# The split of a pair's fourth column sum, issued before or after the next coefficients' split

## The chip, the cores and the metric

The kernel runs on one core of one Trainium2 chip. The metric is the device time of one execution in microseconds, as the median of several runs. A core has five engines that each work through their own list of instructions in order and wait for one another through semaphores: TensorE (PE, with its weight loads shown as PEld), VectorE (DVE), ScalarE (ACT), GpSimd (POOL) and SyncE (SP, which here only issues DMAs).

## What is computed

The reference is a two-layer trunk. Each layer has a token mixer with cross-attention and a layer norm, and then PEER, a channel mixer over 128 x 128 = 16384 experts, with a second layer norm. The change touches only the last part of PEER, the sum over experts of coefficient times value row:

```python
def peer_ffn(x, w_q, subkeys, u_tab, v_tab):
    ...
        gw = jax.nn.softmax(fv, axis=-1)
        u = u_tab[eid]
        act = jax.nn.gelu(jnp.einsum('nhkd,nd->nhk', u, xb).astype(jnp.float32), approximate=False)
        coef = (gw * act).astype(x.dtype)
        return jnp.einsum('nhk,nhkd->nd', coef, v_tab[eid])
```

The kernel doesn't gather rows. It holds a dense coefficient for every expert and token (zero where a token did not pick the expert) and multiplies these coefficients with the whole table `v`, for 256 tokens and 1024 columns.

## The kernel before

**Precision.** A float32 product is made from three products in a shorter type. Each operand is split into a high part (a cast on ACT) and a low part (operand minus high part, a subtraction on DVE), and `mm3` (lines 182 to 186) issues high x high (L184), high x low (L185) and low x high (L186) into one PSUM bank. In the trace every product of the value pass has one of these three lines.

**The value pass** is the loop `for i in range(P)` at line 1276, run once in each of the two layers. Chunk `i` has 128 experts: their coefficients are a block of 128 x 256 (128 experts, 256 tokens), their value rows a block of 128 x 1024. What one turn of the loop issues, in the order in which it is written, is also the order on each engine, since the schedule is manual:

1. `self.next` (line 1279) pumps the split of the value rows two chunks ahead: the cast `wH` on ACT (L110) and the subtraction `wL` on DVE (L125). The pump also issues on SP the DMA that fills the next free raw buffer (L139).
2. `coef(i + 2)` (line 1295) splits the coefficients of the same chunk ahead: the cast `cH` on ACT (L246), the subtraction `cL` on DVE (L247).
3. `paired(i)` (line 1296) does what the pairs below need on ACT and DVE.
4. The products of chunk `i` on PE: for an ordinary chunk four outputs (two token halves by two column halves) of three 128x512 products each. Then come products owed by a pair.

`wH`, `wL`, `cH` and `cL` have three buffers each (`HL_BUFS`), so that the cast of chunk i + 2 into `wH` has to wait until PE is done with chunk i - 1.

**Pairs.** Every six chunks, two neighbouring chunks are multiplied as a 2 x 2 matrix product with seven multiplications instead of eight (the Strassen-Winograd form): `PAIRS` (line 39) lists the first chunk of each pair, 8, 14, ... 98 in layer 0 (16 pairs) and 8, 14, ... 104 in layer 1 (17 pairs). One of the seven products is made in the first chunk's own turn (`m1`, 3 matmuls), two in the second chunk's (6 matmuls). The other four need sums of coefficient blocks and sums of value blocks. `paired` forms these sums on DVE into places of coefficients that are used up, and in later turns splits them: the four coefficient sums into `sh` and `sl`, the four column sums into the tiles `th` and `tl`, which are the first six rows of `xHL`. There are three rows of `th` for four column sums, so the fourth (`t4`) goes into row 0 again once the product that read row 0 is made. The four owed products are three matmuls each and are placed by lines 1242 to 1246: where another pair follows at chunk n, product 0 comes at the end of turn n - 1, products 1 and 2 at the end of turn n, and product 3, the one that uses the fourth column sum, at the end of turn n + 1:

```python
                for m, at in enumerate((n - 1, n, n, n + 1) if n else (p + 4, p + 5, p + 5, p + 5)):
                    owed.setdefault(at, []).append((p, m))
                due[n or p + 5] = p
```

`due` says in which turn the fourth column sum is split: turn n, the first chunk of the next pair, and turn p + 5 behind the last pair of a layer. So it happens 16 times in layer 0 and 17 times in layer 1. In the trace this split is the ACT cast on L1194 and the DVE subtraction on L1195 (both 128x512, writing `xHL`), and product 3 is the group of three matmuls `bank<-xHL` whose second (L185) reads the low part that L1195 writes.

Other lines that the prediction names: L1212 and L1213 are the last two DVE sums of the next pair (in turn n - 1), L1184 a DVE split of a later turn.

Of the kernel before, what the change touches and what calls it, by code (L numbers as in the profile page):

```python
# [50 lines left out]
class Trunk:  # L51
# [986 lines left out]
    def peer_layer(self, layer):  # L1038
        nc, tc, A = self.nc, self.tc, self.A
        with ExitStack() as ctx:  # L1040
# [121 lines left out]
            th, tl = self.xHL[:, 0:3, :], self.xHL[:, 3:6, :]  # L1162
            sh, sl = self.xHL[:, 6, :], self.xHL[:, 7, :]
            plain = lambda a: a.bitcast(F32)
# [4 lines left out]
            def old(p, b, n):  # L1169
                t = lo if p + 6 < CLOSE - 2 else hi  # L1170
                return t[:, b:b + n, :].rearrange("p a b -> p (a b)")

            def sums_c(p):
                return old(p, 0, 2)

            def sums_r(p):
                return [old(p, 2, 4), old(p, 6, 2), old(p, 8 + 2 * (first[p] % 2), 2)]

            def paired(i):
                if i - 2 in first:  # L1180
                    c, (t13, _, _) = sums_c(i - 2), sums_r(i - 2)
                    nc.scalar.copy(sh, c)
                    nc.scalar.copy(th[:, 0:2], t13.rearrange("p (f a) -> p f a", f=2))
                    nc.vector.tensor_sub(sl, c, plain(sh))  # L1184
                if i - 3 in first:
                    t13, t2, _ = sums_r(i - 3)
                    nc.scalar.copy(th[:, 2], t2)
                    nc.vector.tensor_sub(tl[:, 0:2], t13.rearrange("p (f a) -> p f a", f=2), plain(th[:, 0:2]))
                if i - 4 in first:
                    _, t2, _ = sums_r(i - 4)  # L1190
                    nc.vector.tensor_sub(tl[:, 2], t2, plain(th[:, 2]))
                if i in due:
                    _, _, t4 = sums_r(due[i])
                    nc.scalar.copy(th[:, 0], t4)  # L1194
                    nc.vector.tensor_sub(tl[:, 0], t4, plain(th[:, 0]))  # L1195
                if i + 3 in first:
                    (ta, ua), (tb, ub) = part(i + 3), part(i + 4)
                    s = four(sums_c(i + 3))
                    nc.scalar.copy(s[:, 3], ub)
                    nc.vector.tensor_sub(s[:, 1], ta, ua)  # L1200
                    nc.vector.tensor_sub(s[:, 2], ub, s[:, 1])
                    nc.vector.tensor_add(s[:, 0], ua, ub)
                    nc.vector.tensor_sub(ub, tb, s[:, 2])
                if i + 2 in first or i + 1 in first:
                    t13, t2, t4 = sums_r(i + 2 if i + 2 in first else i + 1)
                    t1, t3 = t13[:, :512], t13[:, 512:]
                    (a0, a1), (b0, b1) = [[r[:, :512], r[:, 512:]] for r in self.pair]
                    if i + 2 in first:
                        nc.vector.tensor_sub(t1, a1, a0)
                        nc.vector.tensor_sub(t3, b1, a1)  # L1210
                    else:
                        nc.vector.tensor_add(t2, t3, a0)  # L1212
                        nc.vector.tensor_sub(t4, b0, t2)  # L1213
                        self.n_flight -= 2
                        self.load(len(self.items))
                q = hi[:, 0:2, :].rearrange("p a b -> p (a b)")

                def onto(t, h, src, scale=ALPHA):
                    xs = self.x[:, t, 512 * h:512 * h + 512]
                    nc.vector.scalar_tensor_tensor(xs, xs, scale, src, op0=ALU.mult, op1=ALU.add)  # L1220
                n = i - done
                if n == 1:
                    nc.scalar.copy(q, m1)
                    onto(0, 0, m1)
                elif n == 2:
                    nc.vector.tensor_add(q, q, m6)
                elif n == 3:
                    onto(0, 1, q)
                elif n == 4:
                    onto(0, 1, m5, 1.0)  # L1230
                elif n == 5:
                    nc.vector.tensor_add(q, q, m7)
                elif n == 6:
                    onto(1, 0, q)
                elif n == 7:
                    onto(1, 1, q)
                elif n == 8:
                    onto(1, 1, m5, 1.0)
# [3 lines left out]
            owed, due = {}, {}  # L1242
# [5 lines left out]
            def mixed(out, mh, ml, stat, k=None):  # L1248
                self.mm3(out, *stat, mh, ml, k == PAIRS[layer][0], k == PAIRS[layer][-1])

            def coef(i):
                src = block(i)
                if i in first:
                    cH, cL = cp.tile([P, T], F32R, name="cH"), cp.tile([P, T], F32R, name="cL")
                    self.split_to(cH[:, :P], cL[:, :P], src[:, :P])
                    return cH, cL
                pool, z = (ends, i - P + kept) if layer and i >= P - kept else (cp, "")
                cH = pool.tile([P, T], F32R, name=f"cH{z}")
                cL = pool.tile([P, T], F32R, name=f"cL{z}")
                self.split_to(cH, cL, src)  # L1260
                return cH, cL
# [8 lines left out]
            def products(tt, c0, n, part):  # L1270
                t = slice(tt * P, (tt + 1) * P)
                k, o = divmod(c0, 512)
                for i_, (h, l), (cH, cL) in part:
                    self.mm3(y[tt][k][:, o:o + n], cH[:, t], cL[:, t], h[:, c0:c0 + n], l[:, c0:c0 + n],
                             i_ == 0, i_ == P - 1)
            for i in range(P):
                if i + 2 > P - 1:
                    self.pool_cols = 512
                late.append((i, self.next(min(HL_BUFS, P - i)), cs.pop(0)))
                if i + 2 == CLOSE:  # L1280
                    right.close()
                    if layer == 0:
                        kv = self.later.enter_context(tc.tile_pool(name="kv1", bufs=1, side="right"))
                        self.memctx = self.later.enter_context(ExitStack())
                        m = self.memctx.enter_context(tc.tile_pool(name="mem1", bufs=1, side="right"))
                        self.mem_dest(kv, m)
                        m.tile([P, 80], F32, name="gap")
                        self.kvw = [(m.tile([P, D], F32R, name=f"kH{c}"), m.tile([P, D], F32R, name=f"kL{c}"))
                                    for c in range(4)]
                    else:  # L1290
                        ends = right.enter_context(tc.tile_pool(name="ends", bufs=1, side="right"))
                        self.extra = [(ends.tile([P, D], F32R, name=f"eH{e}"), ends.tile([P, D], F32R, name=f"eL{e}"))
                                      for e in range(EXTRA)]
                if i + 2 < P:
                    cs.append(coef(i + 2))
                paired(i)
                if i + 1 > P - kept:
                    continue
                if i in first or i - 1 in first:
                    (_, (h, l), (cH, cL)), = late  # L1300
                    if i in first:
                        mixed(m1, h[:, :512], l[:, :512], (cH[:, :P], cL[:, :P]), i)
                    else:
                        mixed(y[0][0], h[:, :512], l[:, :512], (cH[:, :P], cL[:, :P]))
                        mixed(y[0][1], h[:, 512:], l[:, 512:], (cH[:, P:], cL[:, P:]))
                else:
                    for tt in range(2):
                        for k in range(2):
                            products(tt, 512 * k, 512, late)
                for p, m in owed.get(i, ()):  # L1310
                    stat = four(sh)[:, m], four(sl)[:, m]
                    if m == 3:
                        mixed(y[1][0], th[:, 0], tl[:, 0], stat)
                    else:
                        mixed((m5, m7, m6)[m], th[:, m], tl[:, m], stat, p)
                late = []
# [175 lines left out]
```

## Time and profile before

| | |
|---|---|
| time, median of 3 runs | 1816.91 us (1815.43 to 1816.98) |
| profiled execution | 1813.94 us, of which the span from first to last instruction is 1812.2 us |
| mean granted TensorE clock | 0.999 |
| bytes moved | 334.24 MB, 184 GB/s over the span |

The value pass is the stretch from about 575 to 850 us (layer 0) and from about 1460 us to the end (layer 1). In a timeline, each row gives the start, the duration, the engine, the line, the operation with what it writes and reads, and in brackets the idle time of the engine ahead of it with what ended that idle time. A view of waits gives who waited for whom, with the total, the number of times and the longest one. The ends of matmuls are modelled, so that their durations overlap; their starts are what shows the rate.

### The profile page before, as it was taken

To read this page: it belongs to the slowest core of one execution; us is meant where nothing else is said; L and a number is where in the kernel's file an instruction comes from. 1 tells how busy PE (TensorE), PEld (TensorE's weight loads), DVE (VectorE), ACT (ScalarE), POOL (GpSimd) and SP (SyncE) were. 2 spreads that over 40 slices of the span, in tenths; PEclk is the share of its full clock that TensorE was granted. 3 is DMA by queue.
4 is the path that set the end of the run, shared out by engine and by line. 5 is a ranking of instruction groups with operands and counts; after the bars stand their busy time and mean duration, and the time that the engine had idled before them with its cause. 6 is when DMAs were issued, how large, how long until landed. Compare 5 with 4: busy or idle time off the path is not lost.

```text
span 1812.2 us, 33806 instructions
## 1 busy us (share of the span) xinstructions
PE 1792.1 (99%) x12711; PEld 1644.4 (91%) x12711; DVE 1489.2 (82%) x3081; ACT 1010.0 (56%) x1781; POOL 430.1 (24%) x324
## 2 busy tenths in 40 slices
PE   8999999999999999999999999999999999999998
PEld 8999999999999788888898899999999988888886
DVE  6684779599998999998868748685999989999977
ACT  6554555455544666666657355555554456666653
POOL 2015762333332000000101368325333300000000
PEclk9999999999999999999999999999999999999999
DMA  7556565655555555665756355665555555555564
GB/s 248 201 160 201 165 199 189 194 174 161 159 162 164 195 193 203 209 202 179 261 178 187 113 177 179 198 191 185 163 162 163 163 186 200 197 192 189 198 200 137
DMA packets 95557, 334.24 MB, mean 184 GB/s; under 512 B 10652, under 2 KB 13728, under 8 KB 95136
## 3 DMA queue, kind: packets, MB, share of 16 engines
q1 hardware_dynamic: 93752, 328.93, 56.6%
q10 hardware_dynamic: 1640, 3.15, 0.5%
q8 instruction: 99, 1.62, 0.4%
q14 instruction: 66, 0.54, 0.1%
HBM read 330.98 MB, written 1.05 MB: 183 GB/s over the span
## 4 chain that ended last, share of the span: by engine, by line
PE 72%; issue 17%; POOL 7%; DVE 2%; ACT 1%; DMA 0%; POOLq 0%; SPq 0%; DVEq 0%; ACTq 0%
PE bank L185 23%; PE bank L186 23%; PE bank L184 23%; POOL wL L120 7%; PE bank L250 2%; ACT wH L110 0%; DVE eL L125 0%; DVE wL L125 0%; PE bank L344 0%; DVE eH L110 0%; POOL wL L123 0%; PE bank L243 0%; DMA cp<-in_rg_par_dram 0%; DMA raw<-in_w0kg_dram 0%; DVE x L297 0%
## 5 line engine op out<-in xcount | busy, mean ns | idle before, releaser
L110 ACT CAST wH<-raw 128x1024 fp32r<-128x1024 f32 (+3 forms) x605 | 612.1, 1013 | 674.8 <-PE bank L186 191.8
L184 PE MATMUL bank<-xHL,wH 128*128 128x256 f32 x2536 | 715.0, 282 | 4.8 <-ACT wH L110 4.8
L186 PE MATMUL bank<-xHL,wL 128*128 128x256 f32 x2536 | 702.2, 277 | 0.5 <-DVE wL L125 0.5
L185 PE MATMUL bank<-xHL,wH 128*128 128x256 f32 x2536 | 702.0, 277 | 0.0
L125 DVE TENSOR_TENSOR wL<-raw,wH 128x1024 fp32r<-128x1024 f32 (+3 forms) x413 | 447.9, 1087 | 236.9 <-ACT wH L110 235.9
L184 PEld LDWEIGHTS bank<-xHL,wH 128*128 128x128 f32 x2536 | 476.9, 188 | 4.8 <-ACT wH L110 4.8
L186 PEld LDWEIGHTS bank<-xHL,wL 128*128 128x128 f32 x2536 | 476.7, 188 | 1.3 <-DVE wL L125 0.7
L185 PEld LDWEIGHTS bank<-xHL,wH 128*128 128x128 f32 x2536 | 477.5, 188 | 0.0
L185 PE MATMUL bank<-wL,cH 128*128 128x512 f32 x850 | 331.1, 390 | 0.4 <-DVE wL L125 0.4
L186 PE MATMUL bank<-wH,cL 128*128 128x512 f32 x850 | 330.5, 389 | 0.0
L184 PE MATMUL bank<-wH,cH 128*128 128x512 f32 x850 | 330.5, 389 | 0.0
L123 POOL TENSOR_TENSOR wL<-raw,wH 128x1024 fp32r<-128x1024 f32 (+1 forms) x121 | 255.6, 2115 | 209.8 <-ACT wH L110 209.1
L120 POOL TENSOR_TENSOR wL<-raw,wH 128x386 fp32r<-128x386 f32 x126 | 129.5, 1028 | 280.1 <-DVE wL L118 280.1
L185 PEld LDWEIGHTS bank<-wL,cH 128*128 128x128 f32 x850 | 159.5, 188 | 34.9 <-DVE wL L125 1.3
L186 PEld LDWEIGHTS bank<-wH,cL 128*128 128x128 f32 x850 | 159.6, 188 | 33.7
L184 PEld LDWEIGHTS bank<-wH,cH 128*128 128x128 f32 x850 | 159.6, 188 | 33.6
L1000 DVE TENSOR_TENSOR oh<-iota,i12T 128x1024 f16<-128x1024 f16 x128 | 130.4, 1019 | 0.0
L333 POOL TENSOR_TENSOR x<-x,raw 128x256 f32<-128x256 f32 x6 | 4.9, 823 | 467.2 <-ACT x L330 467.2
L118 DVE TENSOR_TENSOR wL<-raw,wH 128x640 fp32r<-128x640 f32 x126 | 104.0, 825 | 7.7 <-ACT wH L110 0.3
L1003 DVE TENSOR_TENSOR oh<-oh,gT 128x1024 f16<-128x1024 f16 x128 | 90.0, 703 | 4.4
L1133 PE MATMUL bank<-oh 128*128 128x128 f16 x1024 | 80.9, 220 | 1.1 <-DVE oh L1003 1.1
L1133 PEld LDWEIGHTS <-oh 128*128 128x128 f16 x1024 | 58.8, 97 | 6.0 <-DVE oh L1003 1.5
(339 smaller groups left out, 2122.5 us busy)
## 6 DMA issues: line engine op xcount, KB each, us to landing
raw<-in_u_dram SPq DMA_DIRECT2D x256, 512.0 KB, 3.6
raw<-in_v_dram SPq DMA_DIRECT2D x256, 512.0 KB, 4.5
raw<-in_w_q_dram SPq DMA_DIRECT2D x32, 512.0 KB, 4.2
raw<-in_w_out_dram SPq DMA_DIRECT2D x16, 512.0 KB, 4.0
raw<-in_w0qx_dram SPq DMA_DIRECT2D x8, 512.0 KB, 5.1
raw<-in_wkv_dram SPq DMA_DIRECT2D x8, 512.0 KB, 5.5
raw<-in_w0v_dram SPq DMA_DIRECT2D x8, 384.0 KB, 5.1
raw<-in_w0o_dram SPq DMA_DIRECT2D x8, 384.0 KB, 3.0
```

The lines of the kernel that those rows point to most:

```text
L110: (nc.vector.tensor_copy if self.cast_dve else nc.scalar.copy)(h[:, c], r[:, c])
L118: nc.vector.tensor_sub(l[:, k:], r[:, k:], h[:, k:].bitcast(F32))
L120: nc.gpsimd.tensor_sub(l[:, :k], r[:, :k], h[:, :k].bitcast(F32))
L123: nc.gpsimd.tensor_sub(l[:, :k], r[:, :k], h[:, :k].bitcast(F32))
L125: rest = lambda l=l, r=r, h=h, c=slice(k, n): nc.vector.tensor_sub(l[:, c], r[:, c], h[:, c].bitcast(F32))
L184: mm(out, sH, mH, start=start, stop=False, skip_group_check=True)
L185: mm(out, sH, mL, start=False, stop=False, skip_group_check=True)
L186: mm(out, sL, mH, start=False, stop=stop, skip_group_check=True)
L250: self.nc.tensor.matmul(out, lhsT, rhs, start=start, stop=stop, skip_group_check=True)
L1000: nc.vector.tensor_tensor(flat(oh[:, 1:3]), self.iota2.unsqueeze(1).to_broadcast([P, 4, P, 2]), pairs(self.i12T[:, j]), op=ALU.is_equal)
L1003: nc.vector.tensor_tensor(flat(oh[:, 0:2]), two.rearrange("p z (q e t) -> p z q e t", q=2, t=2), pairs(self.gT[:, j]), op=ALU.mult)
L1133: nc.tensor.matmul(wp[:, qs], oh[:, 2, q // 2, :, q % 2], oh[:, z, q // 2, :, q % 2], start=z == 0, stop=z == 1, skip_group_check=True)
```

## The change

The three statements that split the fourth column sum leave `paired` and go into the loop itself, ahead of `coef(i + 2)`. Nothing else changes: the same instructions with the same operands, in another order.

```diff
@@ in paired(i)
                 if i - 4 in first:
                     _, t2, _ = sums_r(i - 4)
                     nc.vector.tensor_sub(tl[:, 2], t2, plain(th[:, 2]))
-                if i in due:
-                    _, _, t4 = sums_r(due[i])
-                    nc.scalar.copy(th[:, 0], t4)
-                    nc.vector.tensor_sub(tl[:, 0], t4, plain(th[:, 0]))
@@ in the loop over chunks
+                if i in due:
+                    _, _, t4 = sums_r(due[i])
+                    nc.scalar.copy(th[:, 0], t4)
+                    nc.vector.tensor_sub(tl[:, 0], t4, plain(th[:, 0]))
                 if i + 2 < P:
                     cs.append(coef(i + 2))
                 paired(i)
```

The order of each engine's instructions after the change: on ACT, in the 33 turns concerned, `wH`, fourth sum's cast, `cH` instead of `wH`, `cH`, fourth sum's cast; on DVE `wL`, fourth sum's subtraction, `cL` instead of `wL`, `cL`, fourth sum's subtraction. The orders of PE, POOL and SP are the same. Among the waits, the first and third matmul of chunk n + 2 (L184 and L186) now carry waits of their own for `cH` and `cL`; before, the wait of product 3 on the later L1195 had covered them. The subtraction of the fourth sum waits for ACT alone, as before, and its cast waits for PE, as before.

## The prediction

> **What bounds the kernel now.** I read the busy times first, then the waits of PE's weight loads, then the timelines of PE, DVE and ACT around one pair.
>
> ```profile
> span 1812.2 us, 33806 instructions
> PE 1792.1 (99%) x12711; PEld 1644.4 (91%) x12711; DVE 1489.2 (82%) x3081; ACT 1010.0 (56%) x1781; POOL 430.1 (24%) x324
> ```
>
> PE is the bound, so this change can only pay where PE's stream has holes. A modelled matmul end can cover a short hole, so "99%" doesn't say that there are none. The weight loads (PEld) show them better. In their view of waits the longest total is this row:
>
> ```profile
> PEld bank L185 <- DVE xHL L1195: 11.6, 31, 0.4
> ```
>
> L1195 is the moved subtraction. In 31 places PE's second matmul of product 3 waits for it, 0.37 us each (11.6 / 31). There are 33 fourth sums; the two that don't appear are the last of each layer. Now PE's matmuls and weight loads at the first of the 31, and the matmuls at the last:
>
> ```profile
> 615.05 0.40 PE L184 MATMUL bank<-wH,cH 128*128 128x512 f32 x1
> 615.28 0.39 PE L185 MATMUL bank<-wL,cH 128*128 128x512 f32 x1
> 615.51 0.39 PE L186 MATMUL bank<-wH,cL 128*128 128x512 f32 x1
> 615.74 0.40 PE L184 MATMUL bank<-xHL 128*128 128x512 f32 x1
> 616.08 0.50 PE L185 MATMUL bank<-xHL 128*128 128x512 f32 x1
> 616.42 0.40 PE L186 MATMUL bank<-xHL 128*128 128x512 f32 x1
> 616.65 0.40 PE L184 MATMUL bank<-wH,cH 128*128 128x512 f32 x1
> ```
>
> ```profile
> 615.28 0.19 PEld L186 LDWEIGHTS bank<-wH,cL 128*128 128x128 f32 x1
> 615.52 0.19 PEld L184 LDWEIGHTS bank<-xHL 128*128 128x128 f32 x1
> 616.08 0.19 PEld L185 LDWEIGHTS bank<-xHL 128*128 128x128 f32 x1 [0.38 <-DVE xHL L1195]
> 616.19 0.19 PEld L186 LDWEIGHTS bank<-xHL 128*128 128x128 f32 x1
> 616.89 0.19 PEld L186 LDWEIGHTS bank<-wH,cL 128*128 128x128 f32 x1
> ```
>
> ```profile
> 1739.80 0.40 PE L184 MATMUL bank<-xHL 128*128 128x512 f32 x1
> ...
> 1740.72 0.39 PE L184 MATMUL bank<-wH,cH 128*128 128x512 f32 x1
> ```
>
> A group of three without a stall takes 615.74 - 615.05 = 0.69 us, 0.23 each. Product 3 takes 616.65 - 615.74 = 0.91 us at the first place and 1740.72 - 1739.80 = 0.92 at the last. So a stall costs PE **0.22 us**, not the 0.37 of the wait row: the load that waited would have started at about 615.52 + 0.23 = 615.75 and started at 616.08, 0.33 late, but the next load follows after only 0.11 (616.19), so that 0.11 of the delay is made up. All 31 together cost 31 x 0.22 = 6.8 us. Why the subtraction is late, on DVE:
>
> ```profile
> 613.26 0.69 DVE L1213 TENSOR_TENSOR wglo<-raw,wglo 128x512 f32<-128x512 f32 x1
> 613.87 1.22 DVE L125 TENSOR_TENSOR wL<-raw,wH 128x1024 fp32r<-128x1024 f32 x1
> 615.01 0.42 DVE L247 TENSOR_TENSOR cL<-wglo,cH 128x256 fp32r<-128x256 f32 x1
> 615.34 0.69 DVE L1195 TENSOR_TENSOR xHL<-wglo,xHL 128x512 fp32r<-128x512 f32 x1
> 615.94 1.22 DVE L125 TENSOR_TENSOR wL<-raw,wH 128x1024 fp32r<-128x1024 f32 x1
> ...
> 620.68 1.23 DVE L125 TENSOR_TENSOR wL<-raw,wH 128x1024 fp32r<-128x1024 f32 x1 [1.11 <-ACT wH L110]
> ```
>
> DVE works here without a gap. It is behind because the next pair's sums have just been made, and L1195 stands in its queue behind `cL`, which PE needs only later. L1195 ends at 615.34 + 0.69 = 616.03 and PE's load starts 0.05 later.
>
> **The change part by part.**
>
> *DVE.* L1195 goes ahead of `cL`. It can start where `cL` starts now, 615.01, if its input is there, and ends at 615.01 + 0.69 = 615.70, that is 0.33 earlier. With the same 0.05 to PE, the load may start at 615.75, just where it would come without any stall. Even a load at 615.75 + 0.11 = 615.86 would lose nothing, so there is 0.11 us of reserve. The order of two neighbours doesn't change DVE's total: `wL` of the next chunk still starts at 615.94.
>
> *Its input.* The cast on ACT moves ahead of `cH`:
>
> ```profile
> 612.79 0.41 ACT L246 CAST cH<-wglo 128x256 fp32r<-128x256 f32 x1
> 613.10 0.62 ACT L1194 CAST xHL<-wglo 128x512 fp32r<-128x512 f32 x1
> 613.62 1.04 ACT L110 CAST wH<-raw 128x1024 fp32r<-128x1024 f32 x1
> ...
> 619.59 1.05 ACT L110 CAST wH<-raw 128x1024 fp32r<-128x1024 f32 x1 [0.82 <-PE bank L186]
> ```
>
> ```profile
> 612.05 0.39 PE L186 MATMUL bank<-xHL 128*128 128x512 f32 x1
> ```
>
> It would start at 612.79 and end at 613.41, 1.60 us before DVE gets to it. It overwrites row 0 of `th`, which product 0 reads until 612.05 + 0.39 = 612.44; that is 0.35 before 612.79, so its wait for PE still costs ACT nothing. If it did cost something, `cH` and the next `wH` cast would queue behind it, and DVE's `cL` and `wL` behind those. The cast that follows at 613.62 keeps its time.
>
> *What is later.* `cH` starts 0.52 later (613.62 - 613.10), at 613.31, and ends at 613.72, long before DVE's `cL`. `cL` starts 0.60 later (615.94 - 615.34), at 615.61, and ends at 616.03. PE needs it for the load of the third matmul of chunk n + 2, now at 616.89, and 0.22 earlier, at 616.67, once the stall is gone: 0.59 us to spare. That margin is what hides the move; without it PE would stall there. The two new waits on PE for `cH` and `cL` are therefore met when PE comes to them, and I price them at nothing. The nearest row is a load that waited, which started 0.05 after its release; an already met wait has no such delay, and the opposite end, 0.05 at both matmuls of all 33 turns, would be 3.3 us. I take zero, because 0.05 is the price of an operand that comes late, and both operands are there over half a microsecond early.
>
> *Queues.* SP's next DMA goes out when `wL` is done:
>
> ```profile
> 615.12 0.33 SPq L139 DMA_DIRECT2D raw<-in_v_dram  x1
> ```
>
> `wL` ends at 615.09 and comes first in both orders, so no transfer moves. POOL has nothing here, and DVE's 1.11 us of idle at 620.68, ended by ACT and that by PE, shows that the engines start again from PE after each pair: a PE that is 0.22 earlier takes them along and only shortens that idle time.
>
> *The two last fourth sums* (turn p + 5) have no stall to lose; the first of them, and the matmul that reads it:
>
> ```profile
> 851.05 0.68 DVE L1195 TENSOR_TENSOR xHL<-wghi,xHL 128x512 fp32r<-128x512 f32 x1
> ```
>
> ```profile
> 853.32 0.39 PE L185 MATMUL bank<-xHL 128*128 128x512 f32 x1
> ```
>
> It ends at 851.73, 1.59 us early, so being earlier gains nothing.
>
> *Bounds.* The trace doesn't show the subtraction in its new place. At the late end it starts where it does now, 615.34, and the gain is zero. At the early end it starts at 615.01 and the whole stall goes; more than 0.22 per place can't be had from it. I take the early end: in this stretch each DVE instruction starts when its predecessor's row is about to end (615.01 against 613.87 + 1.22 = 615.09), whichever it is, and the input is 1.60 us early. Halfway, at 615.17, the load would come at 615.91, only 0.05 past the reserve. The bounds of the sum are 0 and 31 x 0.22 = 6.8 us.
>
> *A rule that speaks against it.* The Trainium skill, "TensorE: Matmul & The Clock Gate", section "Step-by-step: what each phase is for", says that PE can pull a weight load ahead of matmuls in flight. By that, only the matmul would have waited here, whose turn was 615.97: 0.11 late at 616.08, so the stalls would be worth 31 x 0.11 = 3.4 us in place of 6.8. The trace disagrees: the load of the waiting matmul itself starts at 616.08, and the starts behind it lose 0.22.
>
> **The sum.** 31 x 0.22 = 6.8 us less than the profiled execution's 1813.94 is 1807.1. The median of the runs shown, 1816.91, lies 3.0 above that execution; the change doesn't touch what differs between them, so I forecast 1816.91 - 6.8 = **1810.1 us**.
>
> **Rivals.**
>
> *Half of it.* PE's wait goes only in part: the subtraction reaches PE 0.22 later than worked out (0.33 gained less 0.22 leaves 0.11, and with it half of the stall), or a new wait at chunk n + 2 gives back half. 31 x 0.11 = 3.4, that is 1813.5. For it: PE has two waits that it did not have. Against: reserves of 0.11 and 0.59 us, and the 31 places are alike to a few hundredths in the rows above.
>
> *No change.* The stall only moves: PE comes 0.22 earlier and waits as long for `cL`. For it: `cL` becomes 0.60 later on an engine without a gap. Against: the 0.59 that remain. Or the stall isn't bound to the order: DVE could be held at L1195 by something that the view puts down to nothing. 1816.9.
>
> *Slower.* The cast carries a wait for PE and ACT works in order. If in its new place it were released not by product 0 (612.44) but only after all products of turn n + 1 up to 615.51 + 0.39 = 615.90, it would end at about 616.6, the subtraction at 617.3 and PE's load would start at 617.4 in place of 615.75, 1.65 late, 1.54 after the 0.11: a loss of 1.54 - 0.22 = 1.32 more than now, 31 x 1.32 = 41 us, 1858. It decides from the point at which the cast ends after 615.34 (the old start of the subtraction). Against: now it runs at 613.10, before turn n's products are done, so its wait is for product 0 alone, and PE's order is unchanged.
>
> **How the numbers follow.** Forecast 0.80, half 0.09, no change 0.07, slower 0.04. About 0.2% (3.6 us, a bound at 1813.3) is what a measurement of this kernel can tell from no change. The half lies on that bound and is split evenly: faster 0.80 + 0.04 = 0.84, same 0.05 + 0.07 = 0.12, slower 0.04. The range goes from the profiled execution's 1807.1, a little rounded down for spread, to the half's 1813.5: 1806.8 to 1813.6. It leaves out no change and slower, and the spread of the runs (1.5 us) fits in it.
>
> **What would show it right or wrong.** Right: the view of waits has no row of PEld L185 on the moved subtraction, or one of a few tenths in all; product 3's three starts are 0.23 apart; the subtraction starts right behind `wL` and `cL` 0.60 behind it; DVE's idle time before the L125 after a pair falls from 1.11 to about 0.9; the span is 6 to 7 us shorter. Wrong: PEld waits of similar total on L247 at chunk n + 2 (no change), an ACT row with idle time ahead of the moved cast (slower), or a wait of 0.1 to 0.2 us at the old place (half). A granted clock under the present one would make the prediction wrong for another reason:
>
> ```profile
> 616.00:632.00 16.00, 16.00 (x70) 12.87 (x69) 14.71 (x26) 10.27 (x18) 0.00 (x0) 1.00 0.61 195
> ```

## The result, and the profile after

The changed kernel takes 1809.11 us (median of 7 runs, 1808.74 to 1810.27), the kernel before 1815.43 us (median of 7 runs, 1814.63 to 1816.98). The ratio is 0.9965, with a 95% interval of 0.9954 to 0.9977: 6.3 us less, against the 6.8 forecast (1810.1 us).

First the view of waits of PE's weight loads in the changed kernel, the three rows that name the moved subtraction or what was put behind it:

```profile
PEld bank L184 <- ACT cH L246: 0.8, 1, 0.8
PEld bank L185 <- DVE xHL L1293: 0.3, 1, 0.3
PEld bank L186 <- DVE cL L247: 0.2, 1, 0.2
```

L1293 is the moved subtraction (L1195 before). One wait of 0.3 us is left of 31 that took 11.6 us. The single waits for `cH` and `cL` lie at 1785.92 and 1787.21 us, in a stall near the end that is far from the 33 turns concerned; in those turns no load waits for either. DVE at the first pair:

```profile
615.07 1.22 DVE L125 TENSOR_TENSOR wL<-raw,wH 128x1024 fp32r<-128x1024 f32 x1
616.20 0.69 DVE L1293 TENSOR_TENSOR xHL<-wglo,xHL 128x512 fp32r<-128x512 f32 x1
616.80 0.42 DVE L247 TENSOR_TENSOR cL<-wglo,cH 128x256 fp32r<-128x256 f32 x1
617.14 1.22 DVE L125 TENSOR_TENSOR wL<-raw,wH 128x1024 fp32r<-128x1024 f32 x1
...
621.67 1.23 DVE L125 TENSOR_TENSOR wL<-raw,wH 128x1024 fp32r<-128x1024 f32 x1 [0.90 <-ACT wH L110]
```

The subtraction starts 1.13 us behind the start of `wL`, in the place that `cL` had, and ends at 616.89. The next `wL` starts 2.07 us after the previous one (617.14 - 615.07), as before (615.94 - 613.87), so that the swap costs DVE nothing. The idle time at the end of the burst is 0.90 in place of 1.11. Now PE's weight loads and matmuls at product 3:

```profile
616.72 0.19 PEld L184 LDWEIGHTS bank<-xHL 128*128 128x128 f32 x1
616.94 0.19 PEld L185 LDWEIGHTS bank<-xHL 128*128 128x128 f32 x1
617.18 0.19 PEld L186 LDWEIGHTS bank<-xHL 128*128 128x128 f32 x1
```

```profile
616.94 0.40 PE L184 MATMUL bank<-xHL 128*128 128x512 f32 x1
617.17 0.39 PE L185 MATMUL bank<-xHL 128*128 128x512 f32 x1
617.40 0.40 PE L186 MATMUL bank<-xHL 128*128 128x512 f32 x1
617.64 0.40 PE L184 MATMUL bank<-wH,cH 128*128 128x512 f32 x1
```

The group takes 617.64 - 616.94 = 0.70 us instead of 0.91. It is the same in the other places: over the 31, the group takes 0.90 to 0.92 us in the trace before, and 0.69 or 0.70 in the changed one, but for two of 0.73 and 0.83. The load for L185 at the first place comes 0.22 behind the one ahead of it, at the very moment (616.94) that the subtraction's result can reach PE (616.89 + 0.05).

The mean granted clock is 0.999 in both profiles. The two profiled spans are only 3.7 us apart:

```profile
span 1808.5 us, 33773 instructions
```

The same matmul near the start of the value pass shows where the rest is. It stands twice in each trace, once per layer; first the kernel before, then the changed one:

```profile
600.69 0.50 PE L185 MATMUL bank<-wL,cH 128*128 128x512 f32 x1 [0.22 <-DVE wL L125]
```

```profile
1485.36 0.50 PE L185 MATMUL bank<-wL,cH 128*128 128x512 f32 x1 [0.22 <-DVE wL L125]
```

```profile
601.90 0.50 PE L185 MATMUL bank<-wL,cH 128*128 128x512 f32 x1 [0.22 <-DVE wL L125]
```

```profile
1483.53 0.50 PE L185 MATMUL bank<-wL,cH 128*128 128x512 f32 x1 [0.22 <-DVE wL L125]
```

Up to the first mark, ahead of any changed instruction, the profiled execution of the changed kernel was 1.2 us slower (601.90 - 600.69). From mark to mark it is 884.67 - 881.63 = 3.0 us faster (15 stalls of 0.22 would be 3.3), and from the second mark to the end 326.84 - 324.97 = 1.9 us faster, where 16 stalls would be 3.5. The missing 1.6 are mostly one new wait near the end, on PE in the changed kernel:

```profile
1785.16 0.40 PE L186 MATMUL bank<-wH,cL 128*128 128x512 f32 x1
1785.92 0.50 PE L184 MATMUL bank<-wH,cH 128*128 128x512 f32 x1 [0.36 <-ACT cH L246]
1786.88 0.51 PE L185 MATMUL bank<-wL,cH 128*128 128x512 f32 x1 [0.45 <-DVE wL L125]
1787.22 0.49 PE L186 MATMUL bank<-wH,cL 128*128 128x512 f32 x1
1787.55 0.39 PE L184 MATMUL bank<-eH,cH 128*128 128x512 f32 x1
```

The first two steps are 0.76 and 0.96 instead of 0.23 each, 1.26 us together, and the next two (0.34 and 0.33) add 0.2. More on this stall below.

### The profile page after: what moved, and what is told of

Same layout as the page of the kernel before. It is cut to its first block, busy times and chain, and to the rows that moved or that the text cites. A ratio compares the mean times of both kernels' runs of the same rounds, so it can differ in the third digit from the quotient of the medians.

```text
span 1808.5 us, 33773 instructions
## 1 busy us (share of the span) xinstructions
PE 1788.2 (99%) x12711; PEld 1648.8 (91%) x12711; DVE 1490.7 (82%) x3081; ACT 1010.1 (56%) x1781; POOL 429.8 (24%) x324
## 4 chain that ended last, share of the span: by engine, by line
PE 72%; issue 17%; POOL 7%; DVE 2%; ACT 1%; DMA 0%; POOLq 0%; DVEq 0%; SPq 0%; ACTq 0%
PE bank L186 23%; PE bank L185 23%; PE bank L184 23%; POOL wL L120 7%; PE bank L250 2%; ACT wH L110 0%; DVE eL L125 0%; DVE wL L125 0%; DMA raw<-in_w0kg_dram 0%; PE bank L344 0%; DVE eH L110 0%; POOL wL L123 0%; PE bank L243 0%; DVE x L297 0%; DVE x L318 0%
## 5 line engine op out<-in xcount | busy, mean ns | idle before, releaser
L184 PE MATMUL bank<-xHL,wH 128*128 128x256 f32 x2536 | 715.8, 282 | 4.4 <-ACT wH L110 4.4
L186 PE MATMUL bank<-xHL,wL 128*128 128x256 f32 x2536 | 702.9, 277 | 0.4 <-DVE wL L125 0.3
L185 PE MATMUL bank<-xHL,wH 128*128 128x256 f32 x2536 | 702.8, 277 | 0.0
L184 PEld LDWEIGHTS bank<-xHL,wH 128*128 128x128 f32 x2536 | 477.2, 188 | 4.4 <-ACT wH L110 4.4
L186 PEld LDWEIGHTS bank<-xHL,wL 128*128 128x128 f32 x2536 | 477.2, 188 | 1.2 <-DVE wL L125 0.8
L185 PEld LDWEIGHTS bank<-xHL,wH 128*128 128x128 f32 x2536 | 477.9, 188 | 0.0
L185 PE MATMUL bank<-wL,cH 128*128 128x512 f32 x850 | 331.3, 390 | 0.9 <-DVE wL L125 0.9
L186 PE MATMUL bank<-wH,cL 128*128 128x512 f32 x850 | 330.8, 389 | 0.0
L184 PE MATMUL bank<-wH,cH 128*128 128x512 f32 x850 | 330.3, 389 | 0.4 <-ACT cH L246 0.4
L185 PEld LDWEIGHTS bank<-wL,cH 128*128 128x128 f32 x850 | 159.5, 188 | 35.6 <-DVE wL L125 2.0
L184 PEld LDWEIGHTS bank<-wH,cH 128*128 128x128 f32 x850 | 159.6, 188 | 34.4 <-ACT cH L246 0.8
L186 PEld LDWEIGHTS bank<-wH,cL 128*128 128x128 f32 x850 | 159.6, 188 | 33.7 <-DVE cL L247 0.2
```

The source lines that it names most:

```text
L184: mm(out, sH, mH, start=start, stop=False, skip_group_check=True)
L185: mm(out, sH, mL, start=False, stop=False, skip_group_check=True)
L186: mm(out, sL, mH, start=False, stop=stop, skip_group_check=True)
```

## The experiments

The **theory** is that of the prediction: the subtraction's place in DVE's queue alone made the stall, a delay of its result costs PE what exceeds 0.11 us, and `cL` had 0.59 us to give. Each kernel's time is compared with that of the kernel before, measured beside it on the same chip.

### Which half of the change does it: e1 and e2

The same three statements, with only one engine's order changed. The edit of e1 against the changed kernel:

```diff
-                    nc.scalar.copy(th[:, 0], t4)
-                    nc.vector.tensor_sub(tl[:, 0], t4, plain(th[:, 0]))
-                if i + 2 < P:
+                    c = block(i + 2)
+                    cH, cL = cp.tile([P, T], F32R, name="cH"), cp.tile([P, T], F32R, name="cL")
+                    nc.scalar.copy(cH, c)
+                    nc.scalar.copy(th[:, 0], t4)
+                    nc.vector.tensor_sub(tl[:, 0], t4, plain(th[:, 0]))
+                    nc.vector.tensor_sub(cL, c, plain(cH))
+                    cs.append((cH, cL))
+                elif i + 2 < P:
                     cs.append(coef(i + 2))
```

In e2 the order of the four is: cast of `th`, cast of `cH`, subtraction of `cL`, subtraction of `tl`.

> Only DVE's half of the change: on DVE the fourth sum's subtraction goes ahead of cL, on ACT its cast stays behind cH. Theory (the subtraction's place in DVE's queue is all that matters, and its input was over 1 us early): the cast ends about 613.7 in the time of the first pair before, the subtraction starts at 615.0, so all 31 stalls of 0.22 us go: 6.8 us less than before, ratio 0.9963. Rival A (the earlier cast on ACT makes the gain): no change, ratio 1.000, and the 31 waits of 0.37 us stay.

> Only ACT's half: the cast goes ahead of cH on ACT, on DVE the subtraction stays behind cL. Theory: no change against before, ratio 1.000, with 31 waits of PE on the subtraction of 11.6 us in all as before. Rival A (ACT's order makes the gain): 6 to 7 us less, ratio 0.9963.

Measured: e1 1809.46 us against 1815.68, ratio 0.9965 (0.9951 to 0.9978); e2 1816.11 us, ratio 1.000 (0.9991 to 1.0009). The waits of e1, then of e2:

```profile
PEld bank L185 <- DVE xHL L1296: 0.3, 1, 0.3
```

```profile
PEld bank L185 <- DVE xHL L1297: 11.5, 31, 0.4
```

DVE's order gives the whole gain, ACT's none. Rival A falls.

### How late may it be: e3 and e4

Against the changed kernel, once in e3 and twice in e4:

```diff
                     nc.scalar.copy(th[:, 0], t4)
+                    nc.vector.tensor_add(gl[:, :P], gl[:, P:], gl[:, P:])
                     nc.vector.tensor_sub(tl[:, 0], t4, plain(th[:, 0]))
```

> The changed kernel with one extra DVE addition of 128x128 in front of the subtraction, on a spare tile that nothing reads, at all 33 places: the subtraction comes about 0.21 us later (start to start of such additions in the trace before) than in the changed kernel. Theory (a delay beyond 0.11 us of reserve costs PE one for one): (0.21 - 0.11) x 31 = 3.1 us of the 6.8 come back, 3.7 less than before, ratio 0.998. Rival B (PE loads the weights ahead, so that the reserve is 0.22): nothing comes back, 6.8 less, ratio 0.9963. Rival C (no reserve, every delay counts): 6.5 come back, ratio 0.9998.

> The same with two such additions, the second of which waits for the first: 0.32 + 0.21 = 0.53 us by the dependent and the free step of such additions in the trace before. Theory (reserve 0.11): a loss of 0.42 x 31 = 13.0 us against the changed kernel, so 6.2 us more than before, ratio 1.0034. Rival B (reserve 0.22): 0.31 x 31 = 9.6, so 2.8 more than before, ratio 1.0015. Rival C (no reserve): 16.4, so 9.6 more than before, ratio 1.0053.

Measured: e3 1811.41 us against 1815.68, ratio 0.9977 (0.9968 to 0.9986); e4 1822.37 us, ratio 1.0035 (1.0021 to 1.0049). PE's loads at the second pair, first of e3, then of e4:

```profile
631.91 0.19 PEld L184 LDWEIGHTS bank<-xHL 128*128 128x128 f32 x1
632.34 0.19 PEld L185 LDWEIGHTS bank<-xHL 128*128 128x128 f32 x1 [0.24 <-DVE xHL L1294]
632.45 0.19 PEld L186 LDWEIGHTS bank<-xHL 128*128 128x128 f32 x1
```

```profile
632.87 0.19 PEld L184 LDWEIGHTS bank<-xHL 128*128 128x128 f32 x1
633.62 0.19 PEld L185 LDWEIGHTS bank<-xHL 128*128 128x128 f32 x1 [0.56 <-DVE xHL L1295]
633.73 0.19 PEld L186 LDWEIGHTS bank<-xHL 128*128 128x128 f32 x1
```

And the first matmul of product 3 with the first one behind it, e3 and e4:

```profile
632.13 0.40 PE L184 MATMUL bank<-xHL 128*128 128x512 f32 x1
...
632.90 0.39 PE L184 MATMUL bank<-wH,cH 128*128 128x512 f32 x1
```

```profile
633.09 0.40 PE L184 MATMUL bank<-xHL 128*128 128x512 f32 x1
...
634.20 0.39 PE L184 MATMUL bank<-wH,cH 128*128 128x512 f32 x1
```

The lateness of the load is its distance to the load ahead, less 0.23; the loss is the time of the group, less 0.69. The time against the kernel before is the difference of the two medians:

| kernel | load late, us | loss in one place, us | x 31, us | time against before, us |
|---|---|---|---|---|
| changed | 0.00 | 0.01 | 0 | -6.3 |
| e3 | 0.20 | 0.08 | 2.5 | -4.3 |
| before | 0.33 | 0.22 | 6.8 | 0 |
| e4 | 0.52 | 0.42 | 13.0 | +6.7 |

In all three stalled kernels the loss is the lateness less 0.10 to 0.12, and the times follow it: e4 is 13.0 above the changed kernel in its time, as in the column beside it. The places are alike: the losses of all groups in a trace add up to 2.5 us in e3, 6.9 before and 13.3 in e4. Rival C (no reserve, ratios 0.9998 and 1.0053) is outside both intervals. Rival B (reserve 0.22, 0.9963 and 1.0015) is just outside that of e3 and outside that of e4, and the rows exclude it: by it, a load 0.20 late would lose nothing. In both kernels the waiting load itself is held, as in the kernel before.

### What hides the later coefficients: e5 and e7

Against the changed kernel, extra additions between the subtraction and `coef(i + 2)`, three in e5 (`nc.vector.tensor_add(gl, gl, gl)`) and two small ones in e7, whose edit is:

```diff
                     nc.vector.tensor_sub(tl[:, 0], t4, plain(th[:, 0]))
+                    nc.vector.tensor_add(gl[:, :P], gl[:, P:], gl[:, P:])
+                    nc.vector.tensor_add(gl[:, :P], gl[:, P:], gl[:, P:])
```

> The changed kernel with three extra DVE additions of 128x256, each waiting for the one before, between the fourth sum's subtraction and cL, on a spare tile that nothing reads. They push cL back by about 1.2 us (0.33 free, some 0.45 dependent, from the 0.42 duration of such rows). Theory (cL has 0.59 us in hand and the weight load's 0.11 on top): a stall at the third matmul of chunk n + 2 of about 0.5 us in each place, so 16 us against the changed kernel, 9 to 10 more than before, ratio 1.005. Rival D (cL is nowhere near PE's need, the move costs nothing however late cL is): as the changed kernel, ratio 0.9963.

> The same with two additions of 128x128 behind the subtraction, the pair that took 0.52 us in front of it. Theory: 0.52 is less than the 0.70 that cL has, so nothing is lost: as the changed kernel, 6 to 7 less than before, ratio 0.9963. Rival E (any delay of cL shows on PE, since DVE has no gap there): 0.52 x 31 = 16 more than the changed kernel, ratio 1.005.

Measured: e5 1826.26 us against 1816.75, ratio 1.0054 (1.0040 to 1.0067); e7 1810.04 us against the same, ratio 0.9965 (0.9951 to 0.9978). e5's waits, and then its DVE and its loads at the second pair:

```profile
PEld bank L186 <- DVE cL L247: 22.1, 32, 0.7
```

```profile
633.27 0.42 DVE L1294 TENSOR_TENSOR gl<-gl 128x256 f32<-128x256 f32 x1
...
634.52 0.42 DVE L247 TENSOR_TENSOR cL<-wglo,cH 128x256 fp32r<-128x256 f32 x1
```

```profile
634.09 0.19 PEld L185 LDWEIGHTS bank<-wL,cH 128*128 128x128 f32 x1
634.99 0.19 PEld L186 LDWEIGHTS bank<-wH,cL 128*128 128x128 f32 x1 [0.71 <-DVE cL L247]
```

`cL` is 1.25 us later (634.52 - 633.27) and the load 0.67 (634.99 - 634.09 - 0.23): `cL` had 1.25 - 0.67 = **0.58 us** in hand, 0.59 by the prediction's working. Beyond that and the 0.11 PE pays 0.67 - 0.11 = 0.56 in each place, 17 us in 31; e5 is 15.8 above the changed kernel (9.5 + 6.3). DVE in e7 at the same pair, the first addition and `cL`:

```profile
632.26 0.29 DVE L1294 TENSOR_TENSOR gl<-gl 128x128 f32<-128x128 f32 x1
632.79 0.42 DVE L247 TENSOR_TENSOR cL<-wglo,cH 128x256 fp32r<-128x256 f32 x1
```

Here `cL` is 0.53 later, and nothing is lost: e7's view of PE's weight loads has no row for `cL`. Rivals D and E fall: the cover was real and had the size worked out.

### Still further ahead: e6, and the changed kernel beside it

The split of the fourth sum goes to the top of the turn (and leaves its place in front of `coef(i + 2)`):

```diff
             for i in range(P):
                 if i + 2 > P - 1:
                     self.pool_cols = 512
+                if i in due:
+                    _, _, t4 = sums_r(due[i])
+                    nc.scalar.copy(th[:, 0], t4)
+                    nc.vector.tensor_sub(tl[:, 0], t4, plain(th[:, 0]))
                 late.append((i, self.next(min(HL_BUFS, P - i)), cs.pop(0)))
```

> The fourth sum's split goes still further ahead: before the split of the value rows (wH, wL) of chunk n + 2, at the top of the turn. Theory: the weight load can't come before its turn, and the changed kernel already meets that, so nothing more is gained, ratio 0.9963; ACT now waits about 0.7 us at the cast for product 0, which makes wH about 1.2 later, and DVE's idle time hides it. Rival F (the stall was only partly gone, or more reserve pays): 1 to 3 us less than the changed kernel, ratio 0.995. Rival G (ACT's wait in front of wH costs PE): over 0.2 us in each place, so more than 6 us against the changed kernel, ratio 1.000 or above.

> The changed kernel once more, as the mark for the run that follows it on the same chip. Ratio 0.9965 as before. Its span was only 3.7 us shorter in the first profile, 1.4 us of which was a stall 24 us before the end, behind the last table transfer, one sixteenth of which landed 6.4 us after issue (4.8 before). If that lateness is chance, it is gone in this profile; if it comes with the change, it is there again.

> The split at the top of the turn once more, beside the changed kernel on the same chip. Theory: with no stall left at product 3 in either, both are the same within 0.1%: ratio 0.996 to 0.9965 to the kernel before. Rival F (more reserve pays): over 1.5 us less than the changed kernel in the same call.

Measured: e6 1808.79 us against 1816.75, ratio 0.9957 (0.9943 to 0.9971). The second time, beside the changed kernel: e6's kernel 1808.62 us, ratio 0.9961 (0.9948 to 0.9975), the changed kernel 1808.60 us, ratio 0.9964 (0.9951 to 0.9978), both against 1815.68. The two can't be told apart. The first measurement alone would have left rival F open, since there e6 was 8.0 us below the kernel before and the changed kernel 6.3; the second, with the two side by side, rules it out. The stall near the end is there again in the second profile of the changed kernel (here its PE row), and not in either of e6's:

```profile
1785.24 0.49 PE L185 MATMUL bank<-wL,cH 128*128 128x512 f32 x1 [0.45 <-DVE wL L125]
```

ACT in e6:

```profile
629.37 0.62 ACT L1277 CAST xHL<-wglo 128x512 fp32r<-128x512 f32 x1 [2.10 <-PE bank L186]
629.90 1.04 ACT L110 CAST wH<-raw 128x1024 fp32r<-128x1024 f32 x1
```

The cast now waits at the head of ACT's queue for PE, with `wH` behind it, and the time doesn't show it. In both of its profiles e6 has no wait of PE on the moved subtraction, but the changed kernel had only one to lose. Rivals F and G both fall.

## Why the prediction was right

**What bounds it.** The stalls were worth what the starts of the matmuls said, 0.22 us each, and not the 0.37 of the wait row. By the wait row the gain would have been 11.6 us; it was 6.3 (4.2 to 8.4 by the interval of the ratio).

**DVE.** The subtraction came into `cL`'s place, its result reached PE at the moment it was needed, and 30 of the 31 waits went. e1 shows that this alone makes the gain. The reserve of 0.11, which the prediction took from two loads in one trace, held at three different delays (e3, before, e4).

**Its input.** The cast was early enough in either place (e1), and ACT's order alone changed nothing (e2).

**What is later.** The 0.59 us of cover for `cL` is 0.58 in e5, and the two new waits on PE for `cH` and `cL` cost nothing: in the changed kernel's trace the first group of chunk n + 2, which carries them, takes 0.69 or 0.70 us in all 31 places, as before. e7, where `cL` is still 0.53 later, is as fast as the changed kernel.

**The rule that spoke against it.** The Trainium skill's pull-ahead of weight loads ("TensorE: Matmul & The Clock Gate", section "Step-by-step: what each phase is for") would by estimate have given a loss of 0.42 - 0.11 = 0.31 at e4's places. The rows there lose 0.42: no run here shows a load going ahead of its matmul's missing operand. But the prediction's "The trace disagrees" says too much. In the trace's instruction texts the wait for DVE stands on the load itself in each of the 31 places, before and in e4, and the matmul behind it has none. So the load is held by a wait of its own until the subtraction is done, although what it loads is `sh`, and whether PE would have taken it earlier without that wait was not tested. The price of 0.22 is right for this program either way.

**The sum.** 6.3 instead of 6.8 lies inside what the interval leaves open. The median before moved from 1816.91 to 1815.43 with more runs, 1.5 lower, and the gain came out 0.5 smaller; together the forecast time of 1810.1 was 1.0 too high. In part the two errors cancel, which is luck.

**What did not come.** Of the prediction's signs of being right, one failed: the profiled span was to be 6 to 7 us shorter and was 3.7 shorter, 5.3 in the second profile (1812.2 - 1806.9). The stalls at product 3 did go in that first profile; what is missing is the 1.2 us ahead of any changed instruction and the new stall near the end, of up to 1.5. The prediction's "no transfer moves" holds for the DMA issue that it looked at, and the lateness of the last transfer was in no term of it.

**The rivals.** None of the three came in. The slower one would have needed a late cast; e6, the nearest thing to it, puts ACT's wait in front of the value rows and is still as fast.

## What to carry to other kernels

When two engines feed a third, the order within a burst can set the time even where its total stays the same: look for the operand that is needed first, and put it first, as long as what it passes has that much time in hand. Read the price of a stall from the starts on the bound engine before and behind it, not from the wait row; the difference was a factor of 1.7 here. And work out the reserve of what is moved back (0.59 us here), since beyond it the same swap costs time again, and far enough beyond it becomes a loss (e5, where `cL` is 1.25 later).

## What was not expected

**The length of a weight load.** Its rows say 0.19 us, but behind a late load the next one starts after 0.11 (632.34 and 632.45 in e3). The Trainium skill, "TensorE: Matmul & The Clock Gate", section "LDWEIGHTS (loading the stationary operand)", gives the columns divided by 1.2 GHz, which would be an estimate of 0.107 us for 128 columns; the starts agree with that, the durations of the rows don't.

**A new stall at the end, not settled.** The stall at 1785.92 in the changed kernel stands behind the last transfer of the value table. Its issue on SP:

```profile
1777.77 0.33 SPq L139 DMA_DIRECT2D raw<-in_v_dram  x1
```

By the landings in the trace, the last sixteenth of that transfer arrived at 1784.14, 6.4 us after issue; in the kernel before it took 4.8. In the other profiles it took 6.3 (e1), 4.6 (e2), 5.5 (e3), 4.9 (e4), 6.3 (e5), 5.4 (e7), 5.0 and 4.8 (e6 twice) and 5.8 (the changed kernel again). PE stalls there in the profiles in which it took 5.4 or more, and in no other. In all eleven the ACT cast of that chunk's value rows starts 0.10 or 0.38 us behind the landing, so it is the landing that the stall goes back to. The gain alone doesn't bring it (e5 is slower than the kernel before and has it, e6 is as fast as the changed kernel and doesn't), and it came in both profiles of the changed kernel. What makes the transfer late was not tested and stays open; the stall is worth up to 1.5 us in one execution.
